# A hybrid long-convolution and recurrence block on one core: tiles of pools on released bytes wait for their own bytes alone, and four steps are moved

## The chip, the cores and the metric

The kernel runs on one core of a Trainium2 chip. The metric is device microseconds of one execution, from the first to the last instruction of the program and what lies around them. Engines: PE (TensorE, matmul), PEld (its weight loads), DVE (VectorE), ACT (ScalarE), POOL (GpSimd), SP (SyncE, which here only issues DMAs). DMAs are issued from the queues of SP and ACT.

## What is computed

One layer of a block with two head groups over 4096 latent tokens of width 1024, and 256 context tokens that only feed the recurrence's start. Cut to what matters:

```python
xl = x + grid_sincos(rows, D)
pl = (rms_norm(xl, norm_g) * (1 + sc_l) + sh_l) @ w_in     # 1024 -> 3072 columns: x0 x1 v zh xr zr
u = dwconv(pl[x0,x1,v], 3 taps); y_h = long_conv(v*x1, hyena_filter(4096)) * x0
xc = dwconv(pl[xr], 4 taps); gates = sigmoid(block-diagonal products of xc)
h = forward scan + backward scan of a_t h + b_t            # started from the context's last state
y = [rms_norm(y_h)*silu(zh), rms_norm(h)*silu(zr)] @ w_out
out = rms_norm(xl + g_l * y, final_g)
```

`hyena_filter` is a small network: three layers of 64 with a sine, over the 4096 positions, then a projection to 512 channels and a decay. The long convolution is done as a two-stage DFT of both u = v*x1 and the filter, a product, and the inverse.

## The kernel before

**Precision and tiles.** The large products are made of three f16 matmuls (high by high, high by low, low by high). One column tile of the input projection is 128 columns by 512 tokens and 8 slices of the inner dimension: 24 matmuls of 128x512 into one of three PSUM banks tagged mm. Side products use the tags fa and fb (two banks each) and sm (one).

**Pass A** (`pass_a`, token blocks 0 to 7 upward). Before the loop the modulation (`mod`), the first token block and the weights of xr are loaded and prepared. In each block 12 column tiles are made: xr (4), x1 and v (8). xr goes through the 4-tap convolution and then, by `units_a`, through the forward recurrence; x1*v is stored as u. `tick` closes each column tile: work registered with `at(d, f)` is traced d tiles later. On such steps hang the weight preparation (`wpair`), the context (`ctx_in`, from step CT = 5), the next block's tokens (`xload`, `xsplit`), the filter network (`mlp`, one piece in each of steps 1 to 10), the filter's setup (step FS = 10) and its 16 groups of four rows (`filter_group`, every FD = 4.95 steps).

**Pass B** (`blocks_b`, token blocks 7 down to 0). Column tiles zr, x0, zh (12 a block, in a written order SEQ near the end). zr registers the backward recurrence of its block, `units_b`, whose seven steps lie at the tiles DS after its start: gates (DS[1]), tanh and exponentials (DS[2]), square root (DS[3]), scan and products (DS[4]), sum of squares and scale through PE's `sm` bank (DS[5], `yscale`, tile p2b_yr), split and store of ht (DS[6]). Block 0 has its own list D0. Beside the tiles runs a generator, 1.75 steps a tile: the first DFT stage of u (`s1u_gen`: tiles u, ua, ut, vo), then the second stage with product and inverse for 64 frequencies (`slot_gen`), then the last inverse stage (`inv_block`). Near the end w_out is loaded and scaled in two halves (`wo_load`, `wo_pair`, tile p2b_wo).

**Output** (`phase_out`). `rhalf` multiplies the stored recurrence half (hl) by its half of w_out; `oprep` and `ohalf` do the convolution's half; `ofinal` normalises and stores.

**Order.** The framework schedules at compile time from the traced program: each instruction has the priority of its place, side matmuls (`mms`) 64 places later. Each engine and each DMA queue then runs its list in order.

**Pools.** SBUF pools are opened and closed as a stack on two sides. Later pools lie on the bytes of closed ones: rn on start, flt on ml, rnb and hyb on ap, hy and rn, s1u on flt, slot on s1u, yp on slot, od and o2 on rnb and hyb. As they are opened here, every tile of such a pool waits for every user of the closed pools under it.

Of the kernel before, what the change touches and what calls it, by code (L numbers as in the profile page):

```python
# [10 lines left out]
F32 = mybir.dt.float32  # L11
F16 = mybir.dt.float16
# [10 lines left out]
D = 1024  # L23
# [6 lines left out]
CT = 5  # L30
ML = 1
MK = 1
FS = 10
RQ = 1
OD = 7
OP1 = (0, 0)
RL = 8
IZ = 3
OP2 = 1
OP3 = 2  # L40
PW = ()
IA = (1, 1)
FL = (2, 3)
# [4 lines left out]
MS = ()  # L48
XS = ((1, 1, 2), (1, 2, 3))
PB = {"mm": 3, "fa": 2, "fb": 2, "sm": 1}  # L50
FD = 4.95
XK = ((6, 9), (0, 4))
NX = 11
D0 = (8, 11, 12, 13, 14, 16, 17, 17)
WO = (9, 13, 16)
SEQ = [(2, "zr"), (2, "x0"), (1, "x0"), (1, "zr"), (0, "x0"), (0, "zh"), (0, "zr"), (2, "zh"), (1, "zh")]
XL = [(6, "zr"), (5, "zr"), (4, "zr"), (3, "zr"), (2, "zr"), (1, "x0"), (0, "x0"), (2, "zh")]
DS = (1, 4, 7, 7, 9, 9, 10)
DA = ((12, 14, 15, 15), (4, 4, 6, 6), (3, 5, 6, 8))
EPS = 1e-6  # L60
MAGIC = 1.5 * 2.0 ** 23
# [102 lines left out]
class K:  # L164
# [420 lines left out]
    def pass_a(self):  # L585
        tc, nc, a = self.tc, self.nc, self.a
        with ExitStack() as es, ExitStack() as right:
# [12 lines left out]
            if True:  # L600
                self.columns(sp)
                self.tap_sums()
                m = self.mod(sp, ml, ap, 1)
                next(m)
                self.cpos = ap.tile([128, 512], F32, name="cpos")
                for h in range(2):
                    nc.scalar.dma_start(self.cpos[64 * h:64 * h + 64], a["t_pos"])
                xt = [hy.tile([128, 1028], F32, name="xc", bufs=4)[:, :D] for k in range(3)]
                xr = [self.xload(ap, tok(0), 0, xt[:2], xt[2].rearrange("p (k c) -> p k c", k=2)),
                      self.xload(ap, tok(2), 2)]  # L610
                raw = self.xp_.tile([128, NB, 8, 128], F32, name="X", bufs=2)
                for j in range(NB):
                    nc.sync.dma_start(raw[:, j], a["w_in"][COLS["xr"] + j])
                self.pull(m)
                m = self.mod(sp, ml, ap, 0)
                next(m)
                for k in range(2):
                    self.xsplit(ap, xr[k], self.s1, self.sx, dst(X, 2 * k))
                gs = [self.wprep("xr", j, raw[:, j]) for j in range(NB)]
                for k in range(2):  # L620
                    for j, g in enumerate(gs):
                        W["xr", j] = next(g)
                self.pull(m)
                for g in gs:
                    next(g)

            def wpair(k):
                raw = sp.tile([128, 2, 8, 128], F32, name="wm", bufs=4)
# [6 lines left out]

            def recur():
                sp_.__exit__(None, None, None)
                self.rn = es.enter_context(tc.tile_pool(name="rn", bufs=1))
                self.rnn_consts(self.rn)
                self.carry = [[None] * NB, [None] * NB]  # L640

            def filt():
                self.pull(mlp)
                ml_.__exit__(None, None, None)
                self.flt = right.enter_context(tc.tile_pool(name="flt", bufs=1, side="right"))
                g = self.filter_setup(self.flt)
                next(g)
                for d in FL:
                    self.at(d, lambda: next(g))
            mlp = self.mlp(ml)  # L650
            for k in range(4):
                self.at(k, lambda k=k: wpair(NB + 2 * k))
            self.at(3, recur)
# [2 lines left out]
            ctx = self.ctx_in(ap, hy, W)  # L656
            for d in (0, 2, 4):
                self.at(CT + d, lambda: next(ctx))
            for k in range(10):
                self.at(ML + k // MK, lambda: self.pull(mlp, 1))  # L660
            self.at(FS, filt)
            for n in range(16):
                self.at(FS + FG + int(FD * n), lambda n=n: self.filter_group(self.flt, n))
# [165 lines left out]

    def mlp(self, pool):  # L830
        nc, a = self.nc, self.a
        ws = pool.tile([128, D], F32, name="bm", bufs=1)[:, :384].rearrange("p (l c) -> p l c", l=3)
        nc.scalar.dma_start(ws, a["f_w"])
        fc = pool.tile([128, 6], F32, name="fc")
        nc.vector.tensor_mul(fc[:, 0:3], self.col[:, 104:107], self.col[:, 107:110])
        nc.vector.tensor_copy(fc[:, 3:6], self.col[:, 107:110])
        for half in range(2):
            H = []
            for c in (2 * half, 2 * half + 1):
                z = pool.tile([66, 512], F32, name="x", bufs=4)  # L840
                nc.scalar.dma_start(z, a["t_z"][:, 512 * c:512 * c + 512])
                H.append(z)
            for l in range(3):
                for c in range(2):
                    ps = self.pst("fa" if c % 2 else "fb", 2)
                    self.mms(ps, ws[:66 if l == 0 else 128, l, :], H[c], True, True)
                    x = pool.tile([128, 512], F32, name="x", bufs=4)
                    q = pool.tile([128, 512], F32, name="q", bufs=3)
                    nc.scalar.activation(x, ps, AF.Identity, bias=fc[:, l:l + 1], scale=fc[:, 3 + l:4 + l])
                    nc.vector.tensor_scalar(q, x, INV2PI, MAGIC, op0=OP.mult, op1=OP.add)  # L850
                    nc.vector.tensor_scalar(q, q, -MAGIC, None, op0=OP.add)
                    nc.vector.scalar_tensor_tensor(x, q, -C1, x, op0=OP.mult, op1=OP.add)
                    nc.vector.scalar_tensor_tensor(x, q, -C2, x, op0=OP.mult, op1=OP.add)
                    nc.vector.tensor_scalar(x, x, PI_IN, -PI_IN, op0=OP.min, op1=OP.max)
                    nc.scalar.activation(x, x, AF.Sin)
                    H[c] = x
                yield
            for c in (2 * half, 2 * half + 1):
                h = H[c % 2]
                hl = pool.tile([128, 2, 512], F16, name="q", bufs=3)  # L860
                nc.scalar.activation(hl[:, 0], h, AF.Copy)
                nc.vector.tensor_sub(hl[:, 1], h, hl[:, 0])
                hr = pool.tile([128, 2, 512], F16, name="q", bufs=3)
                nc.vector.tensor_copy(hr, hl[:, :, ::-1])
                lv = hl.rearrange("p x (n m) -> p x n m", m=64)
                rv = hr.rearrange("p x (n m) -> p x n m", m=64)
                n0 = 8 * c
                nc.scalar.dma_start(self.hD[0:64, :, n0:n0 + 8, :], lv[0:64])
                nc.scalar.dma_start(self.hD[0:64, :, 32 + n0:40 + n0, :], lv[64:128])
                nc.scalar.dma_start(self.hD[64:128, :, 25 - n0:33 - n0, :], rv[64:128])  # L870
                k = 7 if c == 0 else 8
                nc.scalar.dma_start(self.hD[64:128, :, 57 - n0:57 - n0 + k, :], rv[0:64, :, 0:k, :])
                if c == 0:
                    nc.scalar.dma_start(self.hD[64:128, :, 0, 1:64], rv[0:64, :, 7, 0:63])
                    nc.scalar.dma_start(self.hD[64:128, :, 0, 0:1], rv[0:64, :, 7, 63:64])
                yield
# [100 lines left out]


    def pass_b(self):
        with self.tc.tile_pool(name="rnb", bufs=1) as rn, self.tc.tile_pool(name="hyb", bufs=1) as hy:  # L980
            self.blocks_b(hy, rn)

    def blocks_b(self, hy, rn):
# [57 lines left out]

    def inv_gen(self):

        yp = self.late.enter_context(self.tc.tile_pool(name="yp", bufs=1, side="right"))
        self.Y = [[yp.tile([128, T], F32, name=f"Y{b}")] for b in range(2)]
        self.Y.append([self.wp.tile([128, D], F32, name="wh", bufs=8) for k in range(4)])
        for b in range(3):
# [74 lines left out]
    def fft_gen(self):  # L1122
        tc, nc, a = self.tc, self.nc, self.a
        self.dn = self.cp.tile([128, 2, 64], F16, name="dn")
        nc.scalar.dma_start(self.dn, a["t_dn"])
        with tc.tile_pool(name="s1u", bufs=1, side="right") as pool:
            st1 = pool.tile([128, 256], F16, name="st1u")
            nc.scalar.dma_start(st1.rearrange("p (h m) -> p h m", h=2), a["t_s1"][0:2].rearrange("h p m -> p h m"))
            yield from self.s1u_gen(pool, st1)
        for b in range(NB):  # L1130
            nc.vector.tensor_scalar(self.cs[:, b:b + 1], self.rl[:, b:b + 1], self.su[b], 128.0, op0=OP.mult, op1=OP.mult)
        with tc.tile_pool(name="slot", bufs=1, side="right") as pool:
            yield from self.slot_gen(pool)

    def s1u_gen(self, pool, st1):

        nc = self.nc
        for j in range(NB):
# [5 lines left out]
            s, self.su[j] = self.pow2(self.cp, tot, 9, 0, f"u{j}", 1)  # L1144
            uv = u.rearrange("c (m n) -> c n m", n=64)
            for q in range(4):
                ua = pool.tile([128, 16, 2, 64], F16, name="ua", bufs=1)
                nc.scalar.activation(ua[:, :, 0, :], uv[:, 16 * q:16 * q + 16, :], AF.Copy, scale=s)
                nc.vector.scalar_tensor_tensor(ua[:, :, 1, :], uv[:, 16 * q:16 * q + 16, :], s, ua[:, :, 0, :],
                                               op0=OP.mult, op1=OP.subtract)  # L1150
                ut = pool.tile([128, 16, 128], F16, name="ut", bufs=2)
                nc.sync.dma_start_transpose(ut, ua.rearrange("c n h m -> c (n h m)"))
                for g in range(4):
                    vo = pool.tile([128, 4, 2, 128], F16, name="vo", bufs=2)
                    ps = self.pst("fa", 2)
                    rhs = ut[:, 4 * g:4 * g + 4, :]
                    self.mms(ps, st1[:, 0:128], rhs, True, False)
                    self.mms(ps, st1[:, 128:256], rhs, False, True)
# [117 lines left out]

    def phase_out(self):
        tc, nc, a = self.tc, self.nc, self.a
        od = self.late.enter_context(tc.tile_pool(name="od", bufs=1))
        self.cpos = od.tile([128, 512], F32, name="cpos")  # L1280
        for h in range(2):
            nc.scalar.dma_start(self.cpos[64 * h:64 * h + 64], a["t_pos"])
# [17 lines left out]
                self.ohalf(xt[self.rd], hrs[c], tt % 4, self.wo[1], self.rrr[:, tt:tt + 1])  # L1300
                self.rd += 1
        rhalf(1)
        o2 = self.o2 = self.late.enter_context(tc.tile_pool(name="o2", bufs=1))
        self.fg = o2.tile([128, D], F32, name="fg")
        nc.scalar.dma_start(self.fg, bcast(a["final_g"]))
        self.Y.append([self.xp_.tile([128, T], F32, name="X", bufs=2)])
# [214 lines left out]
```

## Time and profile before

| | us |
|---|---|
| median of 3 runs | 2239.83 (2232.47 to 2243.20) |
| profiled execution | 2242.97 |
| its span | 2241.2 |
| mean granted TensorE clock | 0.943 |

How to read what follows. In a row of a stage the figures after the length are, for PE, PEld, DVE, ACT and POOL in that order, busy us and instruction count, then PEclk (the mean granted clock, 1 is 2.4 GHz, and the only other level is 1.2 GHz), the mean busy share of the 16 DMA engines and what they moved. In a timeline, square brackets hold the idle time of the engine just before the instruction, and what ended it. A row of a wait list names engine, tile and line that waited, then engine, tile and line that ended it. Line 169 is the helper of all matmuls and line 463 that of additions on POOL, so groups are told apart by their tiles. Names: X is the transposed normalised tokens, wh and wz prepared weights, x and q of line 849 and following the network, vo the first DFT stage's result, p2b a column to be summed over partitions.

### The profile page before, as it was taken

How to read it: one execution, taken by the hardware profiler on the slowest of the kernel's cores; microseconds unless marked ns; L12 is line 12 of the kernel's file. 1: busy time of each engine (PE TensorE's matmuls, PEld its weight loads, DVE VectorE, ACT ScalarE, POOL GpSimd, SP SyncE). 2: the span in 40 equal slices, each digit the busy share in tenths (PEclk: the TensorE clock that was granted, in tenths of full speed). 3: DMA queues.
4: the chain of work that ended last, by engine and by line, in shares of the span. 5: the costliest groups of instructions: out<-in, count | busy, mean ns of one | idle time of the engine just before them, and what ended most of it. 6: DMA issues, size and time to landing. Idle time of an engine off the chain costs nothing. (4 is left out here: it accounts for less than half of the span.)

```text
span 2241.2 us, 30015 instructions
## 1 busy us (share of the span) xinstructions
PE 1934.0 (86%) x10640; PEld 933.0 (42%) x10640; DVE 1362.1 (61%) x2629; ACT 1173.0 (52%) x1828; POOL 623.2 (28%) x417
## 2 busy tenths in 40 slices
PE   6866989989889899878888989898898858999997
PEld 2443434434334344333334545454443434444443
DVE  3894676756647567564543663744745565766576
ACT  2655766664656578576573733744556531432232
POOL 3024344343424321111211342533423300111130
PEclk9987989999999999989999999999999879999999
DMA  9547354565544522666746889889998798344332
GB/s 286 196 123 209 102 184 136 179 171 150 191 126 129 141 90 84 204 184 196 219 147 212 200 202 253 216 217 232 236 234 229 186 264 234 112 143 150 115 125 104
DMA packets 397028, 398.43 MB, mean 178 GB/s; under 512 B 208809, under 2 KB 295359, under 8 KB 392270
## 3 DMA queue, kind: packets, MB, share of 16 engines
q1 hardware_dynamic: 381020, 356.93, 56.4%
q10 hardware_dynamic: 15858, 39.59, 6.0%
q8 instruction: 84, 1.38, 0.3%
q14 instruction: 66, 0.54, 0.1%
HBM read 206.62 MB, written 146.81 MB: 158 GB/s over the span
## 5 line engine op out<-in xcount | busy, mean ns | idle before, releaser
L169 PE MATMUL mm<-X,wh 128*128 128x512 f16 x3072 | 733.4, 386 | 32.2 <-DVE cvx L536 10.2
L169 PEld LDWEIGHTS <-wh 128*128 128x128 f16 x3648 | 325.8, 100 | 455.5 <-issue 93.4
L169 PE MATMUL mm<-X,wz 128*128 128x512 f16 x1536 | 371.9, 389 | 9.8 <-ACT zh L1023 5.0
L169 PEld LDWEIGHTS <-wz 128*128 128x128 f16 x1728 | 158.2, 100 | 226.7 <-issue 58.8
L169 PEld LDWEIGHTS <-hl 128*128 128x128 f16 x1536 | 149.7, 99 | 222.7 <-issue 37.8
L169 PE MATMUL mm<-wz,hl 128*128 128x512 f16 x768 | 176.7, 385 | 18.4 <-DVE oxt L1445 6.9
L169 PE MATMUL mm<-X,hl 128*128 128x512 f16 x768 | 174.7, 382 | 9.5 <-DMA hl<-hlD 9.5
L463 POOL TENSOR_TENSOR acc<-acc,dec 128x512 f32<-128x512 f32 x64 | 88.1, 1377 | 237.2 <-ACT dec L941 227.7
L463 POOL TENSOR_TENSOR oacc<-oacc,osq 128x512 f32<-128x512 f32 x21 | 38.5, 1833 | 330.9 <-ACT oacc L1417 327.8
L466 POOL TENSOR_TENSOR I<-I,xc 128x1024 f32<-128x1024 f32 (+3 forms) x36 | 84.4, 2348 | 161.4 <-ACT I L788 155.0
L169 PE MATMUL fa<-xc,gw 128*128 128x512 f32 (+3 forms) x152 | 79.2, 614 | 46.2 <-DVE cvv L531 19.4
L1201 POOL TENSOR_TENSOR A<-A,B 128x256 f32<-128x256 f32 x64 | 53.1, 829 | 229.1 <-DVE B L1200 194.9
L458 POOL TENSOR_TENSOR xlo<-xt,xh 128x1024 f16<-128x1024 f32 x32 | 74.3, 2344 | 140.1 <-ACT xh L456 140.1
L169 PE MATMUL fb<-tb,vki 128*128 128x128 f16 x768 | 98.2, 225 | 14.6 <-DMA tb<-in_t_s 9.8
L169 PE MATMUL fa<-tb,vu 128*128 128x128 f16 x768 | 97.7, 225 | 0.0
L812 DVE TENSOR_TENSOR_SCAN I<-R,car,I 128x512 f32<-128x512 f32 (+2 forms) x64 | 97.2, 1540 | 0.1
L1212 DVE SCALAR_TENSOR_TENSOR yy<-A,yy 128x512 f16<-128x512 f32 x64 | 56.6, 885 | 64.6 <-ACT yy L1211 64.5
L1199 DVE TENSOR_TENSOR A<-fa,kf 128x512 f32<-128x512 f32 x64 | 43.9, 686 | 81.0 <-ACT kf L1195 78.1
L169 PEld LDWEIGHTS <-vki 128*128 128x128 f16 x768 | 77.2, 101 | 29.5 <-issue 17.9
L466 POOL TENSOR_TENSOR zr<-zr,sg 128x1024 f32<-128x1024 f32 x16 | 39.5, 2466 | 175.7 <-ACT sg L1069 140.9
L169 PE MATMUL fb<-xc,gw 128*128 128x512 f32 (+3 forms) x152 | 77.8, 601 | 10.2 <-ACT I L788 5.0
L463 POOL TENSOR_TENSOR hf<-hf,I 128x1024 f32<-128x1024 f32 x16 | 50.0, 3127 | 129.1 <-DVE I L812 82.2
(345 smaller groups left out, 3420.8 us busy)
## 6 DMA issues: line engine op xcount, KB each, us to landing
VkD<-vk SPq DMA_DIRECT2D x64, 256.0 KB, 2.4
VuD<-vo SPq DMA_DIRECT2D x64, 256.0 KB, 2.6
X<-XD SPq DMA_DIRECT2D x8, 2048.0 KB, 9.6
vu<-VuD SPq DMA_DIRECT2D x128, 128.0 KB, 3.7
vki<-VkD SPq DMA_DIRECT2D x128, 128.0 KB, 3.3
ZD<-zo SPq DMA_DIRECT2D x64, 256.0 KB, 3.5
xt<-in_x SPq DMA_DIRECT2D x30, 512.0 KB, 5.0
xpD<-xt SPq DMA_DIRECT2D x28, 512.0 KB, 3.7
```

Source lines behind the costliest of these rows:

```text
L169: self.nc.tensor.matmul(out, lhsT, rhs, start=start, stop=stop)
L458: nc.gpsimd.tensor_sub(xl, xt, xh)
L463: self.nc.gpsimd.tensor_add(out, x, y)
L466: self.nc.gpsimd.tensor_mul(out, x, y)
L812: nc.vector.tensor_tensor_scan(f(h), f(r), f(h), 0.0 if c is None else c, op0=OP.mult, op1=OP.add)
L1199: nc.vector.tensor_mul(A, u4, kf[:, :, 0:1, :].to_broadcast([128, NB, 2, 64]))
L1201: nc.gpsimd.tensor_sub(A[:, :, 0, :], A[:, :, 0, :], B[:, :, 1, :])
L1212: nc.vector.scalar_tensor_tensor(yy[:, :, 1, :], yv, 0.125, yy[:, :, 0, :], op0=OP.mult, op1=OP.subtract)
```

## The change

- `reuse_waits="tile"` on the pools rn, flt, rnb, hyb, s1u, slot, yp, od and o2: each tile waits for the users of earlier tiles on its own bytes, not for all users of the pools under it.
- The network (`mlp`) is traced ahead of the loop: one piece before the modulation's scale, five before the first `xsplit`, the rest after the weights of xr. Its weights get a tile of their own (`ws`) in place of the bias buffer `bm`.
- The filter starts at step 5 (FS 10 to 5) with a group every 5.2 steps (FD 4.95).
- The first DFT stage of u: two buffers of ua (was one), four of vo (was two), and its results alternate between the banks fb and fa (was fa alone).
- DS is (1, 4, 6, 7, 8, 10, 11), was (1, 4, 7, 7, 9, 9, 10): exponentials, scan one tile earlier, sum of squares and ht one later.
- The two steps of `oprep` come one output tile earlier (OP2 1 to 0, OP3 2 to 1).

```diff
@@ constants
-FS = 10
+FS = 5
-OP2 = 1
-OP3 = 2
+OP2 = 0
+OP3 = 1
-FD = 4.95
+FD = 5.2
-DS = (1, 4, 7, 7, 9, 9, 10)
+DS = (1, 4, 6, 7, 8, 10, 11)
@@ pass_a
+                mlp = self.mlp(ml)
+                self.pull(mlp, 1)
                 self.pull(m)
                 m = self.mod(sp, ml, ap, 0)
                 next(m)
+                self.pull(mlp, 5)
                 for k in range(2):
                     self.xsplit(ap, xr[k], self.s1, self.sx, dst(X, 2 * k))
...
                 for g in gs:
                     next(g)
+                self.pull(mlp)
...
-                self.rn = es.enter_context(tc.tile_pool(name="rn", bufs=1))
+                self.rn = es.enter_context(tc.tile_pool(name="rn", bufs=1, reuse_waits="tile"))
...
-                self.flt = right.enter_context(tc.tile_pool(name="flt", bufs=1, side="right"))
+                self.flt = right.enter_context(tc.tile_pool(name="flt", bufs=1, reuse_waits="tile", side="right"))
...
-            mlp = self.mlp(ml)
...
-            for k in range(10):
-                self.at(ML + k // MK, lambda: self.pull(mlp, 1))
@@ mlp
-        ws = pool.tile([128, D], F32, name="bm", bufs=1)[:, :384].rearrange("p (l c) -> p l c", l=3)
+        ws = pool.tile([128, 3, 128], F32, name="ws")
@@ pass_b (and so for s1u, slot, yp, od, o2)
-        with self.tc.tile_pool(name="rnb", bufs=1) as rn, self.tc.tile_pool(name="hyb", bufs=1) as hy:
+        with self.tc.tile_pool(name="rnb", bufs=1, reuse_waits="tile") as rn, self.tc.tile_pool(name="hyb", bufs=1, reuse_waits="tile") as hy:
@@ s1u_gen
-                ua = pool.tile([128, 16, 2, 64], F16, name="ua", bufs=1)
+                ua = pool.tile([128, 16, 2, 64], F16, name="ua", bufs=2)
...
-                    vo = pool.tile([128, 4, 2, 128], F16, name="vo", bufs=2)
-                    ps = self.pst("fa", 2)
+                    vo = pool.tile([128, 4, 2, 128], F16, name="vo", bufs=4)
+                    ps = self.pst("fa" if g % 2 else "fb", 2)
```

## Rows read from the trace of the kernel before

**Rows 1.** Page, part 1: busy us, share of span, instructions by engine.
```profile
PE 1934.0 (86%) x10640; PEld 933.0 (42%) x10640; DVE 1362.1 (61%) x2629; ACT 1173.0 (52%) x1828; POOL 623.2 (28%) x417
```

**Rows 2.** By stage: stretch, length, engines' busy us (instructions), PEclk, DMA share, GB/s.
```profile
0.00:62.00 62.00, 38.54 (x148) 13.86 (x149) 26.93 (x93) 20.56 (x30) 20.62 (x16) 0.89 1.00 281
62.00:209.00 147.00, 112.94 (x841) 63.25 (x842) 109.28 (x321) 80.35 (x142) 32.98 (x20) 0.89 0.55 159
...
313.00:408.00 95.00, 84.72 (x349) 37.30 (x348) 66.38 (x110) 60.62 (x103) 43.62 (x27) 0.95 0.62 201
...
991.00:1097.00 106.00, 87.97 (x368) 39.18 (x367) 61.13 (x94) 67.84 (x88) 28.40 (x13) 0.92 0.62 187
...
1818.00:1852.00 34.00, 8.02 (x147) 6.81 (x145) 20.41 (x47) 9.55 (x14) 0.00 (x0) 0.57 0.99 297
```

**Rows 3.** Timeline of PE, starts of token blocks 0 to 3: start, us.
```profile
61.98 4.01 PE L169 MATMUL mm<-X,wh 128*128 128x512 f16 x11 [0.34 <-DMA X<-xh]
...
208.56 1.46 PE L169 MATMUL mm<-X,wh 128*128 128x512 f16 x3 [8.90 <-DMA X<-xh]
...
313.03 1.24 PE L169 MATMUL mm<-X,wh 128*128 128x512 f16 x5
...
407.86 0.38 PE L169 MATMUL mm<-X,wh 128*128 128x512 f16 x1
```

**Rows 4.** Waits of PE, 62:209: us in total, times, longest us.
```profile
PE mm L169 <- DMA X<-xh: 9.2, 2, 8.9
PE mm L169 <- DVE xc L536: 7.1, 1, 7.1
PE fa L169 <- ACT R L788: 6.5, 1, 6.5
PE fb L169 <- ACT x L855: 4.4, 2, 2.3
...
PE fa L169 <- ACT x L855: 2.4, 2, 1.4
```

**Rows 5.** Tile x (network): duration ns min/median/max, first and last start us.
```profile
L169 PE MATMUL fb<-x,bm x12: 590/592/1153, 83.6 to 152.5; 128*128 128x512 f32 x8, 66*128 66x512 f32 x4
...
L850 DVE TENSOR_SCALAR q<-x x12: 410/418/427, 85.5 to 157.8; 128x512 f32<-128x512 f32 x12
...
L853 DVE SCALAR_TENSOR_TENSOR x<-q,x x12: 681/683/2487, 88.8 to 160.6; 128x512 f32<-128x512 f32 x12
```

**Rows 6.** Busy time in the second half of loading and late in block 0.
```profile
31.00:62.00 31.00, 17.74 (x77) 6.86 (x78) 20.02 (x63) 16.79 (x24) 13.96 (x7) 0.83 1.04 264
...
115.00:168.00 53.00, 35.91 (x269) 21.68 (x267) 49.91 (x147) 27.41 (x49) 15.18 (x8) 0.87 0.51 129
```

**Rows 7.** Timeline of ACT at the handover of pass A to pass B.
```profile
907.09 0.78 ACT L1016 ACTIVATE zr<-mm,be,es 128x512 f32<-128x512 f32 x1 [3.99 <-DVE cva L555]
```

**Rows 8.** Waits over the whole span: us in total, times, longest us.
```profile
PE sm L169 <- DVE p2b_yr L190: 28.8, 5, 9.4
...
ACT vo L1160 <- DMA VuD<-vo: 23.0, 10, 5.5
...
PE fa L169 <- DVE vo L1161: 21.3, 12, 5.3
```

**Rows 9.** Timeline of PE at the seam: start, us, instruction, idle before.
```profile
1779.67 0.16 PE L169 MATMUL sm<-p2b_yr,onesb 128*128 128x1 bf16 x1 [9.44 <-DVE p2b_yr L190]
...
1842.71 0.16 PE L169 MATMUL sm<-p2b_wo,onesb 128*128 128x1 bf16 x1 [8.47 <-DVE p2b_wo L190]
1852.36 28.34 PE L169 MATMUL mm<-X,hl 128*128 128x512 f16 x120 [9.48 <-DMA hl<-hlD]
```

**Rows 10.** Queues of ACT and SP at the seam: start, us, issue.
```profile
1842.35 1.90 SPq L1407 DMA_DIRECT2D oz<-zD  x4
...
1843.54 0.61 ACTq L1382 DMA_DIRECT2D hl<-hlD  x1
```

**Rows 11.** Tile ht: who waited for it, us in total and times.
```profile
  ACT zr L1016: 4.1, 2
```

More of the change, by code (lines that the diff above doesn't have):

```diff
@@ L1042, in inv_gen @@
     def inv_gen(self):
-        yp = self.late.enter_context(self.tc.tile_pool(name="yp", bufs=1, side="right"))
+        yp = self.late.enter_context(self.tc.tile_pool(name="yp", bufs=1, reuse_waits="tile", side="right"))
         self.Y = [[yp.tile([128, T], F32, name=f"Y{b}")] for b in range(2)]
@@ L1125, in fft_gen @@
         nc.scalar.dma_start(self.dn, a["t_dn"])
-        with tc.tile_pool(name="s1u", bufs=1, side="right") as pool:
+        with tc.tile_pool(name="s1u", bufs=1, reuse_waits="tile", side="right") as pool:
             st1 = pool.tile([128, 256], F16, name="st1u")
@@ L1131, in fft_gen @@
             nc.vector.tensor_scalar(self.cs[:, b:b + 1], self.rl[:, b:b + 1], self.su[b], 128.0, op0=OP.mult, op1=OP.mult)
-        with tc.tile_pool(name="slot", bufs=1, side="right") as pool:
+        with tc.tile_pool(name="slot", bufs=1, reuse_waits="tile", side="right") as pool:
             yield from self.slot_gen(pool)
@@ L1278, in phase_out @@
         tc, nc, a = self.tc, self.nc, self.a
-        od = self.late.enter_context(tc.tile_pool(name="od", bufs=1))
+        od = self.late.enter_context(tc.tile_pool(name="od", bufs=1, reuse_waits="tile"))
         self.cpos = od.tile([128, 512], F32, name="cpos")
@@ L1302, in phase_out @@
         rhalf(1)
-        o2 = self.o2 = self.late.enter_context(tc.tile_pool(name="o2", bufs=1))
+        o2 = self.o2 = self.late.enter_context(tc.tile_pool(name="o2", bufs=1, reuse_waits="tile"))
         self.fg = o2.tile([128, D], F32, name="fg")
```

## Prediction

> **What bounds the kernel now.** I read the busy table first: TensorE (PE) is busy 86% of the span, DVE 61%, ACT 52% [rows 1]. Then busy time by stage, cut where a token block starts, because the share of the whole span hides which stage leaves PE idle: the load phase (0 to 62 us) is at the DMA engines' limit, share 1.00; the first block (62 to 209) keeps PE busy 112.9 of 147 us at a granted clock of 0.89, while a steady block (313 to 408) holds 0.95; the seam before the output phase (1818 to 1852) has PE busy 8 of 34 us at 0.57 [rows 2]. The block starts make that concrete: block 0 takes 208.56 - 61.98 = 146.6 us, block 2 takes 407.86 - 313.03 = 94.8 us [rows 3]. The third view is the list of what PE waited for, by stage. The chain of waits shows only the final norm and store and was of no use. So the time is PE work plus some 307 us in which PE is idle (2241.2 - 1934.0) and stretches at half clock; the change has to be priced as idle time taken out of named stages. The profiled execution took 2242.97 us (span 2241.2 and 1.8 around it), 3.1 above the median of 2239.83; the sum below is made against 2242.97 and 3 is taken off at the end.
>
> **A. The network (mlp) into the load phase, filter from step 5 on, pools rn and flt by tile.** Of the 34 us that PE idles in block 0, 4.4 + 2.4 are waits for the network's sine, 7.1 for the convolution on DVE, 9.2 for the next block's transposed X and 6.5 for the gate sigmoid [rows 4]. The network's own work in it: 12 layer matmuls of two records each; with 0.59 us a record, overlapping, I take 0.9 a matmul, 11 us of PE. On DVE, 12 times three operations of 0.42 and two of 0.68, so 31 us [rows 5], in a stretch where DVE is busy 49.9 of 53 us; in 31 to 62 us it is busy 20 of 31 [rows 6]. So DVE paces the later part of block 0, and the chain context -> free xt buffers -> x load -> X that ends it. Moving 31 us of DVE away is worth more than the 6.8 us of waits that bear its name. Floor: block 0 as long as block 2 plus about 10 for the context's projection and the eight weight preparations that only it has: 105, a gain of 42. Against it stand the filter's setup and about one group of four rows (roughly 6 us of PE) which now fall into it, and the X chain, which is still serial. Lower bound: no gain. I take 24, nearer to the floor's middle, since DVE is the named pacer. In the load phase ACT, DVE and PE have room; its DMA does not. The network reads 0.2 + 0.5 MB and its first half writes 1 MB there: 1.7 MB at 281 GB/s [rows 2] is 6 us if none of it hides; half on the path, -3. The queue it is put on is ACT's, where positions and bias rows are issued; behind them wait only loads that are needed after 30 us. A: 21, from -10 to 42.
> The Trainium skill has a rule against this move (DMA: Bandwidth & Descriptors, section Issuing engines are not separate DMA queues): a DMA issued by ACT ends up on the same 16 engines as SP's. By that rule the whole 6 us would be on the path, and the sum would end 3 higher; the DMA share of 1.00 in this stretch does not contradict it.
>
> **B. Handover of pass A to pass B (rnb, hyb, s1u by tile).** The first eviction of the gate columns waits 3.99 us on ACT and so starts only when DVE is through with the last unit of pass A: the pool-wide wait [rows 7]. PE has three banks ahead and loses little of it. Bounds 0 and 6 (the wait, and the FFT's first loads behind it on SP); I take 3. For slot, yp and o2, whose first loads need the previous stage's stores anyway, I take 0, bounds -2 and 4.
>
> **C. First DFT stage of u in four banks.** PE waits 21.3 us in 12 places for DVE's low half of vo, which frees bank fa; ACT in turn waited 23.0 us in 10 places for vo buffers still being stored [rows 8]. Both are doubled (vo 2 -> 4, fa only -> fa and fb, ua 1 -> 2). No instruction is added. Cost: the recurrence's gates use fb as well, so a gate matmul may now find it held. Bounds 0 and 21; I take 15.
>
> **D. Last recurrence steps spread.** PE waits 28.8 us in 5 places for p2b_yr, the sum of squares that ends the recurrence unit [rows 8]; the unit's scan and this sum are in the same step (9, 9). After: scan at 8, sum at 10, so two more column tiles lie between, and a tile is 106 / 12 = 8.8 us long [rows 2], more than any of these waits. The longest, 9.44, is that of token block 0, which comes last [rows 9], and whose steps are in another list and stay. So 28.8 - 9.4 = 19.4 are open; I take 17. What comes later: the store of ht (step 10 -> 11) and so the release of zr, which the next unit's first tiles overwrite at step 12; see the third rival.
>
> **E. Seam to the output phase (od by tile).** PE waits 8.47 us for p2b_wo and then 9.48 for hl [rows 9]. hl was issued on ACT's queue at 1843.54, and SP's load of the output gate at 1842.35 [rows 10], both right after the second half of w_out was squared into a buffer of the old pools (its sum is the p2b_wo of 1842.71): the wait for the old pools' last users. Most of od lies on the recurrence's pool, whose last unit took its sum at 1779.67 [rows 9], over 60 us before. With hl there, rhalf can start when the last inverse DFT before the seam ends; it needs only the already prepared half of w_out. Bounds 0 (issue order unchanged) and 18; I take 14, because p2b_wo's own chain (load, scale, square) is unchanged and may still stand in PE's queue somewhere. The output preparation one tile earlier (OP2, OP3): the same work, 0, bounds -3 and 4.
>
> **F. Clock.** The stretches at 1.2 GHz follow such gaps: the seam has 0.57, block 0 0.89 [rows 2]. At 0.57 about 0.86 of 34 us is at half clock, and of the 8 us of PE work in it some 4 are lost; for C and D, whose gaps of 5 to 7 us are followed by the same, I put another 4. F: 8, bounds 0 and 20.
>
> **Sum.** 21 + 3 + 15 + 17 + 14 + 8 = 78. Gaps that close let the next wait on the same matmul become visible: in block 0 alone five different releasers share the idle time [rows 4]. I take back a quarter: 58. 2242.97 - 58 = 2185, less 3: **2182 us**.
>
> **Rivals.** (1) The pools by tile don't do what they say: loads keep their place in the queues because they are issued in the same order, so E and B and the X chain in A don't move. What is left is 10 (A) + 15 + 17 + 4 = 46, three quarters of it 35: 2205. For it: the order of issue within a queue is fixed in the program. Against: the issue comes within 2 us of the end of the old pools' last user [rows 10].
> (2) The network blocks the start. Each of six double layers runs PE, ACT, five DVE operations, ACT in series, some 6 us [rows 5]; were PE's modulation matmuls queued behind each, the first projection would start up to 36 us later. Block 0 would still be shorter. A becomes about -10: 78 - 31 = 47, three quarters 35, the same 2205.
> (3) Slower than before: zr is held. Now ACT's eviction into zr already waits 4.1 us in 2 places for the ht step [rows 11]. With ht one tile later it could wait in each of the seven units. PE has three banks, so it decides from the point where ht's second half ends more than two tiles after the eviction is due. If PE then loses one tile (8.8 us) in each of 7 units, that is 62 us; D's share of the gain (13 after the quarter) is gone too: 2182 + 13 + 62 = 2257. Against it: the ht step itself is short, and two tiles of slack are 17 us.
> (4) Better than forecast: block 0 falls to its floor (42), C, D and E give all (21, 19, 18), F 12, B 6, start -3: 115, so 2125.
>
> **How the numbers follow.** Forecast (2155 to 2215) 0.60; rivals 1 and 2, 2195 to 2228, together 0.20; better (2120 to 2155) 0.10; rival 3 (2240 to 2270) and what lies between it and the others 0.10. The range from 2138 to 2232 leaves out most of rival 3 and half of the better case. A measurement of this kernel tells about 0.5% (11 us) from no change, so faster is below 2228.6: 0.87; within 2228.6 to 2251: 0.07; slower: 0.06.
>
> **What would show it.** A: layer matmuls of the network before 62 us, first projection at 60 to 68, second block starting near 185 instead of 208.56; wrong if block 0 stays above 140. C: PE's wait for vo under 7 us. D: PE's wait for p2b_yr near 10, one place. E: hl issued before 1840 on the old scale and no wait of 9 us before the first output matmul; wrong if the seam has the two waits still. Rival 3: ACT zr waiting for ht in most units. The forecast is wrong as a whole if PE's idle total falls by less than 30 us.

## The result, and the profile after

| | before | after |
|---|---|---|
| median, us | 2236.15 (2231.22 to 2243.20, 4 runs) | 2179.72 (2177.39 to 2180.86, 4 runs) |
| ratio, 95% interval | | 0.9747 (0.9720 to 0.9774) |
| span of the profiled execution, us | 2241.2 | 2179.1 |
| mean granted TensorE clock | 0.943 | 0.943 |

The change makes the kernel 2.5% faster, 57 us; the forecast was 2182. The total came out as forecast, but hardly any of its terms did, and most of what follows is about that.

One caution for all that is read below from single traces. The runs of the kernel before that were made beside these lie between 2227.99 and 2243.2, and its profiled execution (2242.97) is at the upper end. By that spread I take it that a stage that differs by under some 6 us between two traces says little by itself.

The busy table of the changed kernel, which answers to [rows 1]:

```profile
PE 1922.3 (88%) x10640; PEld 931.4 (43%) x10640; DVE 1364.5 (63%) x2629; ACT 1170.6 (54%) x1827; POOL 609.3 (28%) x417
```

PE's idle time fell from 307 to 257 us, its busy time from 1934 to 1922 over the same 10640 matmuls.

By stage, cut at the changed kernel's own block starts; columns as in [rows 2]. The last line is the output phase from the first matmul of the convolution's half on:

```profile
0.00:79.00 79.00, 48.38 (x165) 16.98 (x165) 48.96 (x141) 31.22 (x48) 20.86 (x16) 0.84 0.95 276
79.00:210.00 131.00, 109.02 (x845) 60.83 (x845) 90.72 (x287) 74.57 (x134) 36.03 (x24) 0.93 0.52 151
314.00:406.00 92.00, 83.52 (x342) 36.58 (x341) 58.76 (x104) 53.16 (x93) 44.72 (x27) 0.96 0.63 201
964.00:1064.00 100.00, 85.84 (x361) 38.23 (x359) 58.01 (x82) 64.55 (x85) 27.41 (x12) 0.91 0.63 184
1784.00:1810.00 26.00, 4.57 (x99) 3.67 (x97) 17.31 (x38) 9.28 (x14) 0.00 (x0) 0.64 1.02 342
...
1869.00:2170.00 301.00, 298.35 (x1407) 137.87 (x1407) 208.45 (x449) 95.67 (x147) 41.83 (x29) 0.99 0.39 134
```

PE's timeline at the starts of token blocks 0 to 3 (answers to [rows 3]):

```profile
79.22 0.59 PE L169 MATMUL mm<-X,wh 128*128 128x512 f16 x1 [12.06 <-DMA X<-xlo]
...
210.06 0.82 PE L169 MATMUL mm<-X,wh 128*128 128x512 f16 x3 [4.47 <-DMA X<-xh]
...
313.98 1.24 PE L169 MATMUL mm<-X,wh 128*128 128x512 f16 x5
...
406.30 0.38 PE L169 MATMUL mm<-X,wh 128*128 128x512 f16 x1
```

The first projection starts 17 us later than before (79.22 against 61.98), block 0 is 16 shorter (130.8 against 146.6), and the second block starts where it did, 1.5 us later. The gain lies elsewhere: blocks 1 to 7 take 666 us (681), pass B 908.5 (928.8), the seam from the last column to the first output product 26 (34), the output phase from there to its last matmul 359 (380).

The waits of PE over the whole span (us in total, times, longest), cut to those of the forecast's terms:

```profile
PE sm L169 <- DVE p2b_yr L190: 14.8, 4, 10.5
...
PE sm L169 <- DVE p2b_wo L190: 8.8, 1, 8.8
...
PE mm L169 <- DMA hl<-hlD: 7.5, 1, 7.5
```

The wait for vo, 21.3 us in [rows 8], is gone but for 1.5 us in fa and 1.0 in fb. The wait for p2b_yr is halved. Both waits of the seam are still there.

### The profile page after: what moved, and what is told of

Read it like the earlier page. It is cut to its first block, busy times and chain, and to the rows that moved or that the text cites. A ratio compares the mean times of both kernels' runs of the same rounds, so it can differ in the third digit from the quotient of the medians.

```text
span 2179.1 us, 29936 instructions
## 1 busy us (share of the span) xinstructions
PE 1922.3 (88%) x10640; PEld 931.4 (43%) x10640; DVE 1364.5 (63%) x2629; ACT 1170.6 (54%) x1827; POOL 609.3 (28%) x417
## 5 line engine op out<-in xcount | busy, mean ns | idle before, releaser
L169 PE MATMUL mm<-X,wz 128*128 128x512 f16 x1536 | 366.2, 385 | 2.8 <-DVE cva L555 2.8
L169 PEld LDWEIGHTS <-hl 128*128 128x128 f16 x1536 | 150.4, 99 | 200.4 <-DMA hl<-hlD 16.5
L463 POOL TENSOR_TENSOR oacc<-oacc,osq 128x512 f32<-128x512 f32 x21 | 32.6, 1553 | 299.6 <-ACT oacc L1418 296.6
L805 DVE SCALAR_TENSOR_TENSOR xc<-xh,xc 128x1024 f32<-128x1024 f32 (+2 forms) x34 | 49.2, 1448 | 69.2 <-ACT xh L802 60.2
```

Source lines behind the costliest of these rows:

```text
L169: self.nc.tensor.matmul(out, lhsT, rhs, start=start, stop=stop)
L463: self.nc.gpsimd.tensor_add(out, x, y)
L805: nc.vector.scalar_tensor_tensor(Z, M, 1.0, Z, op0=OP.add, op1=OP.mult)
```

## The experiments

Four kernels undo one part of the change each, three move the network or the filter, two take DVE work out, two move the seam's loads, and one puts a single part into the kernel before. A difference of 0.001 in the ratio is 2.24 us; each ratio is good to about 0.0025 either way, so differences under some 8 us are not resolved.

| kernel | median us | ratio to before (95%) | beside after (0.9747), us |
|---|---|---|---|
| pools as before | 2183.76 | 0.9776 (0.9753 to 0.9799) | +6.5 |
| OP2, OP3 as before | 2192.90 | 0.9817 (0.9793 to 0.9841) | +15.7 |
| DS as before | 2180.57 | 0.9771 (0.9744 to 0.9799) | +5.4 |
| first DFT stage as before | 2195.01 | 0.9821 (0.9796 to 0.9847) | +16.5 |
| network and filter as before | 2193.78 | 0.9819 (0.9799 to 0.9839) | +16.1 |
| filter alone as before | 2191.30 | 0.9798 (0.9785 to 0.9811) | +11.4 |
| network behind X | 2182.57 | 0.9758 (0.9738 to 0.9778) | +2.5 |
| squares of w_out behind hl | 2177.36 | 0.9746 (0.9724 to 0.9768) | -0.2 |
| after, less DVE work | 2170.34 | 0.9721 (0.9696 to 0.9745) | -5.8 |
| network and filter as before, less DVE work | 2182.37 | 0.9775 (0.9750 to 0.9799) | +6.3 |
| before with new DS | 2237.59 | 1.0015 (1.0003 to 1.0028) | |
| hl and oxt ahead of the squares | 2176.37 | 0.9758 (0.9734 to 0.9782) | +2.5 |

The five undos that don't overlap (pools, OP, DS, DFT stage, network with filter) add up to 60 us, beside the 57 of the whole change.

### Pools as before

```diff
-... reuse_waits="tile" ...)      # on all nine pools
+... )
```

> The changed kernel with every pool opened as before (all tiles wait for all users of the closed pools under them); everything else as changed, and the order of instructions on every engine is the same, so waits alone differ. By the forecast's terms E (14), B (3) and a part of A for the X chain go, three quarters of some 18 to 22: 2180 + 15 = about 2195. By the rival that a load keeps its place in its queue: within 5 of 2180, the seam with the same two waits of 7 to 9 us.

Measured: 2183.76, 6.5 us by the ratio, and the two intervals overlap. The handover keeps its wait in the changed kernel: ACT's timeline there (answers to [rows 7]), with the same releaser as before:

```profile
892.37 0.78 ACT L1017 ACTIVATE zr<-mm,be,es 128x512 f32<-128x512 f32 x1 [2.97 <-DVE cva L555]
```

And with the pools as before, the seam is 27.3 us long, against 25.9. So what the pools release early is worth between nothing and some 14 us, and the two places where I had put 17 us for them (B and E) are not among it. The other reading, that a load keeps its place in its queue, fits.

### The output preparation one tile later again

```diff
-OP2 = 0
-OP3 = 1
+OP2 = 1
+OP3 = 2
```

> The changed kernel with the output preparation's steps one tile later again (OP2 1, OP3 2). By the forecast's term (0, from -3 to 4) it stays within 4 of 2180. By the two traces, whose output phases differ by 20 us (379.6 and 359.2 between first and last output matmul) while the seam's waits only moved, these two constants carry that gain: 2195 to 2200, and PE waits for oxt and hl in the output phase come back.

Measured: 2192.90, +15.7 us. This edit, which I had priced at nothing, is one of the three largest. Its place is seen by cutting the output phase at the first matmul of the convolution's half, to the last matmul: before, then with OP2 and OP3 undone; the changed kernel's line (301 us long, PE busy 298.35) stands above.

```profile
1911.00:2232.00 321.00, 303.01 (x1407) 137.34 (x1407) 207.04 (x448) 95.03 (x147) 47.66 (x29) 0.99 0.36 126
```

```profile
1860.00:2180.00 320.00, 302.41 (x1407) 137.41 (x1407) 207.91 (x449) 95.29 (x147) 47.11 (x29) 0.99 0.37 126
```

The same 1407 matmuls take 320 or 301 us. What PE waited for in this stretch, in the kernel before:

```profile
PE mm L169 <- DVE oxt L1445: 6.9, 4, 2.0
PE mm L169 <- DVE hl L1431: 4.7, 8, 0.7
PE mm L169 <- DVE wh L1445: 3.6, 2, 2.2
PE mm L169 <- ACT hl L1430: 3.3, 2, 1.8
```

and in the changed kernel, where little is left:

```profile
PE mm L169 <- ACT hl L1431: 1.8, 1, 1.8
PE mm L169 <- DVE oxt L1446: 0.8, 1, 0.8
...
PE mm L169 <- DVE hl L1432: 0.3, 1, 0.3
```

With the steps one tile later the four waits are back (6.7, 4.5, 3.3 and 2.9 us). Idle PE accounts for 15 of the 20 us between before and after (321 - 303 against 301 - 298.35), and PE's own busy time for 4 to 5.

### The recurrence's steps, undone and alone

```diff
-DS = (1, 4, 6, 7, 8, 10, 11)
+DS = (1, 4, 7, 7, 9, 9, 10)
```

> The changed kernel with the recurrence's steps DS as before. By the forecast's term D (17, three quarters 13): about 2193, with PE waiting 25 to 29 us for p2b_yr. By the waits that the changed kernel has in its place (p2b_yr still 14.8, p2t_yr 4.0, ACT's zr waiting for the ht store 21.0): a gain of 5 or less, so 2180 to 2185.

> The kernel before with the new recurrence steps DS alone. The forecast's term D: 17, three quarters 13: about 2223 beside 2236. By the undo of the same constants in the changed kernel, which cost nothing: 2232 to 2240, with the waits for p2b_yr down from 28.8 to about 15 and as much more in other waits of pass B. A gain here of 10 with none there would say that D and the banks take away the same idle time.

Measured: undone in the changed kernel +5.4 us, not resolved; alone in the kernel before it costs 3 us (0.7 to 6.3). The wait it aims at does what the forecast says. With the old steps in the changed kernel it is

```profile
PE sm L169 <- DVE p2b_yr L190: 36.5, 5, 9.9
```

and 14.8 in 4 places with the new; it is 28.8 in the kernel before, 10.4 with the new steps in it. But pass B doesn't get less idle. Pass B by the windows view, the kernel before, then the same with new steps:

```profile
889.60:1818.40 928.80, 803.33 (x5047) 412.49 (x5046) 510.63 (x829) 512.30 (x737) 270.00 (x200) 0.95 0.79 210
```

```profile
890.20:1815.30 925.10, 798.03 (x5094) 411.69 (x5092) 514.95 (x836) 514.42 (x739) 269.47 (x200) 0.94 0.80 212
```

PE is idle 125.5 and 127.1 us in them, and in the changed kernel 106.6 with the new steps (next section) and 107.0 with the old. Pass B's waits of the kernel before with the new steps show where the 18 us went:

```profile
PE fa L169 <- DMA ut<-ua: 10.6, 3, 8.7
PE fa L169 <- DVE vo L1161: 10.4, 7, 3.5
PE sm L169 <- DVE p2b_yr L190: 10.4, 2, 6.7
...
PE fa L169 <- DMA oz<-ZD: 8.2, 2, 6.8
...
PE mm L169 <- ACT zr L1016: 5.9, 2, 5.1
PE fa L169 <- DVE Y L1272: 5.9, 1, 5.9
```

In the kernel before these were 1.9, 21.3, 28.8, 2.7, 0.9 and 0.6. PE then waits for the generator's DMAs, for zr and for the inverse's DVE work instead: the idle time has several owners that stand behind each other. Even the wait for vo, at which another part of the change aims, halves with these steps alone, and PE is no less idle.

What the new steps do shorten is the seam: with them it is 25.9 us long in the changed kernel and 27.1 in the kernel before, with the old ones 32.0 and 34.0. Behind the last column stand four groups of the last inverse stage's matmuls (fa<-dn, 24 each) with the new steps, six with the old, in every kernel here. So 6 to 7 of the 8 us by which the seam fell go with DS and not with the pools. Those two groups only move in among the columns, and little of this is left in the totals.

### The first DFT stage as before

```diff
-ua ... bufs=2; vo ... bufs=4; ps = self.pst("fa" if g % 2 else "fb", 2)
+ua ... bufs=1; vo ... bufs=2; ps = self.pst("fa", 2)
```

> The changed kernel with the first DFT stage as before (one ua, two vo, bank fa alone). By the forecast's term C (15, three quarters 11): about 2191, with 15 to 21 us of PE waiting for vo. If the gates, which use bank fb as well, gave most of it back (their waits rose from 18.5 + 5.0 to 22.3 + 8.7), 2183 to 2186.

Measured: +16.5 us, with the wait back where it was, PE's first line of pass B:

```profile
PE fa L169 <- DVE vo L1162: 22.1, 13, 3.9
```

Pass B takes 924.8 us and PE is idle 125.5 of them; in the changed kernel:

```profile
875.90:1784.40 908.50, 801.86 (x5095) 413.66 (x5094) 513.41 (x835) 510.26 (x737) 266.72 (x200) 0.94 0.81 216
```

That is 106.6 idle, so 18.9 us less, against 19.6 us less waiting for vo. Here what PE is spared stays spared; the gates that share bank fb gave back little. Bank, vo and ua were undone together, so which of them does it isn't separated.

### Network and filter

```diff
 # network and filter as before          # filter alone as before
-self.pull(mlp, 1) ... self.pull(mlp, 5)
+at(ML + k, pull(mlp, 1)), k in 0..9
-FS = 5;  FD = 5.2                        -FS = 5;  FD = 5.2
+FS = 10; FD = 4.95                       +FS = 10; FD = 4.95
```

> The changed kernel with the network in the column steps 1 to 10 and the filter from step 10 on, as before; pools, banks, steps and output preparation as changed. By the forecast's term A (21, three quarters 16) it is slower: about 2196, first projection at 62, second block at 208. By the traces (the start lost 17, block 0 won 16, blocks 1 to 7 won 15): if the 15 hang on when the filter runs, 2194; if they come from the pools or the banks, 2180 or less.

> The changed kernel with the network first as changed, but the filter from step 10 on (FS 10, FD 4.95). If block 0's 131 us and blocks 1 to 7's 666 come from the network alone, the times of the changed kernel stay (2180). If the filter's earlier and slower spread carries the 15 us of blocks 1 to 7, these go back to 681 and block 0 gets shorter by the group of filter rows that it no longer holds (6): 2188.

> The changed kernel with the network traced behind the first token block's X and xr's weights, still ahead of the column tiles (the pieces ahead of the modulation and of the first split are taken from there). If the 17 us later first projection is DVE, ACT and the x loads serving the network ahead of X (rival 2), it comes back to 62 to 66 and the pieces reappear in block 0 beside the columns: block 0 135 to 145, total 2168 to 2176. If the start is held by something else, the first projection stays near 79 and the total at 2180 or above.

(The third takes out the two early pulls, so that the whole network is traced behind xr's weights.) None of the three undoes the network's place whole: all keep its weights in their own tile ws. These are loaded at 17.87 us in the kernel with network and filter as before (61.51 in the kernel before, where they stood in the buffer bm), and its first layer runs in the load phase, though it is traced at step 1:

```profile
26.15 2.05 PE L169 MATMUL fb<-x,ws 66*128 66x512 f32 x2 [3.98 <-DMA x<-in_t_z]
```

Of the network's 24 matmul records 8 start ahead of the first projection there, 10 with the network behind X, 16 in the changed kernel, none in the kernel before [rows 5]. Starts by PE's timeline, us:

| | first projection | second block | pass B |
|---|---|---|---|
| before | 61.98 | 208.56 | 889.59 |
| network and filter as before | 65.74 | 204.75 | 883.21 |
| filter alone as before | 78.94 | 204.40 | 880.67 |
| network behind X | 68.71 | 208.73 | 869.62 |
| after | 79.22 | 210.06 | 875.92 |

With the filter late in both, the network's place in the program moves the first projection by 13 us and block 0's length by as much the other way (139.0 and 125.5); the second block starts at 204.4 or 204.8, and the totals differ by 2.5 us in the medians and 4.7 by the ratios, unresolved. With the network behind X the start comes back to 68.71, later than the 62 to 66 that I had named, and the total does not fall. So moving the network from a third to two thirds ahead of the first projection is worth about nothing; what the first third is worth, no run shows. What the filter's earlier start is worth is 11.4 us. By the two traces it is paid in block 0 (5.4 us more) and won in blocks 1 to 7 (10.4 less); another 4.5 lie in pass B, by themselves too little to be told from chance. Blocks 1 to 7, filter late, then the changed kernel:

```profile
204.40:880.70 676.30, 612.31 (x2653) 271.63 (x2654) 443.76 (x829) 440.95 (x738) 251.34 (x152) 0.96 0.48 146
```

```profile
210.00:875.90 665.90, 608.63 (x2640) 271.78 (x2641) 447.92 (x825) 436.07 (x733) 243.06 (x148) 0.96 0.48 147
```

PE is busy 3.7 us less and idle 6.7 us less. The first group of filter rows lies in block 0 now: up to 320 us the filter's tile kd feeds 22 matmuls in the changed kernel, from 163.5 us on, and 16 in the kernel before, from 250.9 on. The groups are now one tile in 5.2 and not in 4.95; one wait hints that they meet fewer of the convolution's evictions (PE for cvv, 18.7 us in 3 places with the filter late, 9.2 in 2 with it early). Whether it is the distance or the offset of five tiles wasn't separated. The filter's setup needs the network's result, so the network's early place may be what lets the filter start at step 5; no run has the early filter with the late network.

### Less DVE work in the network

```diff
-nc.vector.tensor_scalar(q, x, ...); nc.vector.tensor_scalar(q, q, ...)
-nc.vector.scalar_tensor_tensor(x, q, -C1, ...); nc.vector.scalar_tensor_tensor(x, q, -C2, ...)
```

> The changed kernel without the network's range reduction: four of its five DVE operations a layer and half are left out (12 times 0.42 + 0.42 + 0.68 + 0.68, 26 us of DVE; the filter's values are not the reference's). If DVE, busy 28 of 31 us before the first projection, is what delays it, the first projection goes from 79 to 62 to 68 and the total falls by 10 to 15: 2165 to 2170. If the delay comes from the loads of the network or from PE and ACT taking turns on its layers, the start stays at 75 to 79.

> The kernel with the network in steps 1 to 10 and the filter from 10 on, again without the four DVE operations a layer. The forecast priced DVE's 26 to 31 us out of block 0 at 24 us: block 0 from 139 to 115 to 118, the second block from 205 to 181 to 185, the total from 2194 to about 2172. If block 0 is paced by the chain from the next block's tokens to X, or by PE's own columns, it gets shorter by 8 or less.

With the network in its old steps, taking 26 us from DVE (10 of the network's 24 matmul records lie ahead of block 0 there, 8 without this edit) shortens block 0 from 139 to 122 us, and the second block starts at 188.3 instead of 204.8: 17 of the 24 us that I had priced. The total falls by 10. With the network first, the same work taken out moves the first projection only from 79.22 to 74.70. So DVE isn't the only one that holds the start, and the trace of that kernel names the other. DVE, the last piece of the first tokens:

```profile
50.19 1.27 DVE L454 SCALAR_TENSOR_TENSOR xt<-xt,rq_x,s 128x1024 f32<-128x1024 f32 x1
```

ACT, which has to split this piece (xh, L456) before it can be transposed:

```profile
53.73 0.56 ACTq L864 DMA_DIRECT2D hD<-q  x1
54.33 0.62 ACTq L865 DMA_DIRECT2D hD<-q  x1
55.05 0.92 ACTq L866 DMA_DIRECT2D hD<-q  x1
56.00 0.90 ACTq L868 DMA_DIRECT2D hD<-q  x1
56.94 1.19 ACTq L870 DMA_DIRECT2D hD<-q  x1
58.17 1.18 ACTq L871 DMA_DIRECT2D hD<-q  x1
59.40 0.63 ACT L857 ACTIVATE q<-x 128x512 f16<-128x512 f32 x1 [5.48 <-DMA hD<-q]
...
65.44 1.99 ACT L456 ACTIVATE xh<-xt 128x1024 f16<-128x1024 f32 x2
```

The piece is ready at 51.5 and split at 65.4: ten stores of the network's result, issued by ACT, and the network's activations stand ahead of it in ACT's list. In the changed kernel both are at work; its last piece on DVE and its last split, then the last split of the kernel before:

```profile
61.85 1.27 DVE L454 SCALAR_TENSOR_TENSOR xt<-xt,rq_x,s 128x1024 f32<-128x1024 f32 x1
...
68.39 1.04 ACT L456 ACTIVATE xh<-xt 128x1024 f16<-128x1024 f32 x1
```

```profile
55.08 1.06 ACT L456 ACTIVATE xh<-xt 128x1024 f16<-128x1024 f32 x1 [0.61 <-DMA X<-xh]
```

DVE is done with its piece at 63.1 (8 us past the old start of the split), and ACT comes 5.3 us after that, having issued six stores of hD between 61.96 and 67.81. The other 4 of the 17 us lie behind the split: the first projection follows it after 10.8 us, 6.9 before. With the network behind X the last split is back at 55.01, and the start is still 6.7 us late. So the splits aren't all of it: in that kernel network operations stand on DVE from 56 to 64 us, and the scaling of xr's weights (L484, 64.09) comes behind them. That a store from another queue would bring the start forward is argued from the lists; no run moved the stores.

### The seam

```diff
 # squares of w_out behind hl
-    nc.scalar.activation(junk, w, AF.Square, ...)   # in wo_load(0)
+    # the same four, traced in phase_out behind rhalf(1)
 # hl and oxt ahead of the squares
+hrs[7] = self.hload(od, 7); load(4); (four squares); (cpos); rhalf(1)
```

> The changed kernel with the four squares of w_out's second loaded half taken out of its load step and traced behind the first recurrence product of the output (into orp's buffer), so that on ACT's list they stand behind cpos and hl instead of ahead of them. If hl is late because of its place behind these squares (rival 1's reason), hl is issued near 1788 instead of 1802, the first output matmul follows the last inverse DFT near 1797 instead of 1810, and the total falls by 5 to 12: 2168 to 2175. If hl waits for the bytes of the old pools, it is issued at 1802 as before and the time stays at 2180.

> The changed kernel with hl and the first four output tiles' loads issued ahead of the four squares of w_out's second loaded half, and cpos behind them. When the squares alone were moved, hl was issued 11 us after the last column instead of 18, the seam fell from 25.9 to 20.4, and the output phase gave 11 back through late oxt loads (DVE waiting 7.4 for one). If that is how it was lost, the seam is 16 to 20 here, the output phase near 360, and the total 2168 to 2174. If hl is held by the bytes of the old pools, or PE only meets w_out's sum later, the time stays at 2177 to 2181.

Issues of ACT's queue at the seam in the changed kernel (answers to [rows 10]): hl still behind the last square of w_out.

```profile
1801.04 1.06 ACT L1359 ACTIVATE zh<-wh 128x1024 f16<-128x1024 f32 x1 [0.45 <-ACT zh L1359]
...
1802.29 0.61 ACTq L1383 DMA_DIRECT2D hl<-hlD  x1
```

With the squares behind it, hl is issued at 1783.76, 10.8 us after the last column instead of 17.9, and the seam is 20.4 us long; with the oxt loads ahead too, 16.1. So hl was late because of its place in ACT's list. But neither kernel is measurably faster. The first matmul of the convolution's half, in the changed kernel, with the squares moved, and with the loads moved too:

```profile
1869.25 1.04 PE L169 MATMUL mm<-wz,hl 128*128 128x512 f16 x2 [1.76 <-ACT hl L1431]
```

```profile
1862.93 1.46 PE L169 MATMUL mm<-wz,hl 128*128 128x512 f16 x3 [1.50 <-ACT hl L1435]
```

```profile
1876.71 1.89 PE L169 MATMUL mm<-wz,hl 128*128 128x512 f16 x4 [1.50 <-ACT hl L1437]
```

Their last columns end at 1784.42, 1772.97 and 1789.92, so this matmul comes 84.8, 90.0 and 86.8 us later. In each kernel exactly 192 matmuls of the recurrence's half lie ahead of it, and from here to the end it is 310 us in all three. In the two kernels with the short seam its end isn't what bounds this stretch: the matmul comes 69.5 and 70.7 us after it. In the other twelve kernels, with seams of 25.2 to 34.0 us, it comes 58.2 to 59.8 us after it, so there a longer seam goes with a longer stretch (92.9 us from the last column to this matmul in the kernel before). With 192 matmuls to fill it, a gap made shorter than that comes back as a longer one among or behind them. What sets the stretch then is probably the chain through the last inverse DFT, the second half of w_out and the first output preparation; that is read from these lengths, and no run shortened the chain itself.

## Why the prediction was right, point by point

The total was right because errors cancelled. By the undos, beside the terms of the forecast before its quarter was taken back:

| term | forecast | measured |
|---|---|---|
| A, network and filter | 21 | 16.1: the network's place in the program 5 or less, the filter's start 11.4; its own weight tile not undone |
| B and E, pools | 17 | 6.5, not resolved from 0, and not at the handover or the seam |
| C, four banks | 15 | 16.5 |
| D, steps | 17 | 5.4 undone, not resolved; -3 alone |
| OP2, OP3 | 0 | 15.7 |
| F, clock | 8 | not isolated: the mean granted clock is 0.943 in both |

**A** had the right size for the wrong reason. Three of its steps failed. The start was priced at 3 us and cost 17: I looked for cost on the DMA engines (their share fell from 1.00 to 0.95 in the longer load phase), and it came from DVE and ACT, whose room in 31 to 62 us I had read from their busy shares (20 and 17 of 31, [rows 6]) without asking what stood behind the network in their lists. The sentence "behind them wait only loads that are needed after 30 us" counted the DMAs on ACT's queue and forgot that ACT's own splits of X stand in the same list. Rival 2 described this in kind, up to 36 us, through PE; it happened through ACT and DVE. The second block "near 185" came only when DVE's work was really left out (188.3); moved, the work was paid in the load phase. That the tile ws lets part of the network run there by itself I had not priced at all. And the filter, which I had counted as a cost of 6 us in block 0 (the traces have 5.4 there), was the gain, mostly in blocks that I had not priced at all.

The rule I weighed there (the Trainium skill, DMA: Bandwidth & Descriptors, section Issuing engines are not separate DMA queues) says besides that the sequencer's time to start a DMA is usually small relative to the DMA itself. That agrees with the kernel before: its issues of hD take 0.5 to 1.0 us, and the three whose landing the trace tells land 2.5 to 5.3 us after their start. But in the changed kernel each issue of hD takes 0.5 to 1.3 us of ACT's list, and the six ahead of the last split take 4.4 together, which is not small where ACT's next instruction is on the path.

**C** was right in mechanism, size and the sign to look for (PE's wait for vo 2.5 us in all, forecast under 7).

**D** was right in mechanism and wrong in worth. The wait fell as forecast (to 14.8 in 4 places; I had said about 10 in one), but I took its 17 us as PE time, and about 5 were, if any. The rule I applied, a quarter back for the next wait, is far too little where several chains (gates, generator, zr) are late by about the same. Rival 3, zr held by ht in every unit, did not happen: ACT waited for it 5.9 us in 4 places, against 4.1 in 2. (The 21.0 us that I named ahead of the undo are ACT's wait for the store of an earlier ht before it writes the next one, not zr's.)

**E** was wrong in its cause, and the criterion that I had set for that ("the two waits still there") was met. Rival 1 had the right reason. The seam did get 8 us shorter, but mostly by DS, which I had not connected with it. That a still shorter seam wouldn't have been a gain either, because something else then bounds the first matmul of the convolution's half, no view that I had read could tell.

**F** can't be read off. PE is busy 11.7 us less in the changed kernel, but the other twelve kernels, all with parts of the change, lie anywhere from 1912 to 1926 us, and 4.7 of the 11.7 are in the output phase at the same granted clock of 0.99. Time at 1.2 GHz is 2 x (1 - 0.943) of the span, some 255 us before and 248 after. That the gaps of C and D are followed by half clock was assumed; no run isolates it. What F may be worth is contained in the undos of the other lines.

**OP2 and OP3** were priced at 0 with "the same work", and the waits of 6.9, 4.7, 3.6 and 3.3 us in the output phase were not looked at. They were in the trace of the kernel before.

The sum shows how the errors met: A, B with E, D and F (as a line of its own) were too high by 5, 10.5, 11.6 and 8, together 35; C and the output preparation too low by 1.5 and 15.7; and 20 of the 78 had been taken back. 78 - 35 + 17 is 60, beside the 58 that I had kept. That these met within 2 us was luck.

**Open.** Where the pools' 6.5 us lie, if they are there. Whether the filter gains by its offset or its distance. What the network's own weight tile is worth. Which part of the first DFT stage's edit does it. Whether storing hD from another queue than ACT's gives the start 5 us back; it wasn't tried. No kernel here that does the whole work is measurably faster than the changed one.

## To carry to other kernels

Price an edit that only moves a step in the stage where the step is consumed: look up what PE waits for there before writing 0. Moving work out of a full stretch gains only if nothing on the path stands behind it where it goes, and for an engine that also issues DMAs its whole list counts, computing and issuing together. An undo that leaves one tile of the change in place may leave the move itself half done: look in the trace where the work ran, not only where it was traced. A wait that is one of several of like size gives back its time only as far as the next one is earlier; undoing that one part alone, in both kernels, is the way to see it.

## What the runs showed of the hardware

ACT's time per issued store in the changed kernel, 0.5 to 1.3 us for the pieces of hD at a DMA share of 1.04 (60 to 72 us), is of the order of its computing instructions there (0.6 to 1.1 us). The same 1407 matmuls of the output phase were busy 302 to 303 us in the two kernels whose output preparation stands one tile later, where PE was idle 18 us in short pieces between them, and 298 in the changed one, where it was idle 3, at a granted clock of 0.99 each time.
